# A two-layer hybrid trunk: three 256-column matmuls per weight block in place of a 512-column and a 256-column one, and no folds

## Chip, cores and metric

The kernel runs on one core of one Trainium2 chip. The metric is the device time of one execution in microseconds, from start to end; less is better. Three runs of the kernel before took 2072.51 to 2072.72 us, with a median of 2072.55 us.

## What is computed

Two residual layers on a stream x of 256 positions by 2048 features, in float32. The first mixes tokens by sparse attention over the keys that an indexer selects, the second by a gated short convolution; behind each stands a dense MLP with a squared ReLU. Cut to what matters here:

```python
x = x + dsa_mixer(rmsnorm(x), attn_w_in, attn_w_out)      # 2048 -> 4176, 2048 -> 2048
x = x + sqrelu_mlp(rmsnorm(x), mlp_w1[0], mlp_w2[0])      # 2048 -> 8192 -> 2048
x = x + short_conv_mixer(rmsnorm(x), conv_w_in, conv_w_out)  # 2048 -> 6144, 2048 -> 2048
x = x + sqrelu_mlp(rmsnorm(x), mlp_w1[1], mlp_w2[1])
```

Nearly all the work is in the products of activations with weights. All 389 MB of weights are read once.

## The kernel before

**Precision.** TensorE takes float32 operands in a fast form (fp32r). To keep accuracy, each operand is cut in two: a high part, the value rounded to that form, and a low part, what is left. A product is the sum of three: high by high, high by low and low by high. `split` (lines 215 to 237) does this for the weights: a ScalarE copy makes `wh` (line 231), a VectorE subtraction makes `wl` (line 232). Activations lie transposed, features on partitions; for each feature tile k there is a 512-column row `xk` with the 256 positions' high parts in columns 0 to 255 and their low parts in columns 256 to 511.

**Units, ticks and pieces.** The work is a fixed list of units, made by `add_unit` (lines 189 to 195) in the order of lines 942 to 1002. A unit is one strip of a weight matrix (up to 1104 columns wide) with its whole or partial contraction. It runs in ticks; each tick takes one piece, `kk` feature tiles of the strip. The main loop (lines 1059 to 1072) issues the matmuls of one piece, lets every live generator take one step (`step_all`; the generators are the ends of earlier units, norms, attention), and splits a later piece; the splits run four pieces ahead. The order of instructions on every engine is the order in which this Python code issues them.

**Wide units** (query, key, value and indexer projections, and the very last strip) hold a 128-position tile of the activations as the stationary operand and move 336 to 512 weight columns past it: three matmuls for each product, lines 258 to 260.

**Tall units**, all others, 116 of them, hold a 128x128 weight block as the stationary operand and move activations past it. Each has four blocks of columns, and a PSUM bank of 512 columns for each block. For each block and feature tile there are two matmuls:

```python
nc.tensor.matmul(o, wh, xk, start=(k == 0), stop=False)
nc.tensor.matmul(o[:, 0:256], wl, xk[:, 0:256], start=False, stop=(k == K - 1))
```

The first (line 253) moves all 512 columns past `wh`, so the bank's first half collects high by high and its second half high by low. The second (line 254) moves the 256 high columns past `wl` into the first half. There are 5248 such pairs (2816 with activations in the tile `xp`, 2432 in `hq`).

**Folds.** When a unit ends, the halves of its four banks are added: `fold` (lines 835 to 839) copies the second half to SBUF on ScalarE (tile `half`) and adds the first half to it on VectorE. `fold4` (lines 841 to 850) does it for the four banks, two in a step, and gives two SBUF tiles of 512 columns. Five ends call it: `add_to_xT` (the residual add), `h_gen` (squared ReLU), `c_end`, `y_gen` and `by_gen` (the convolution's three inputs). There are 464 folds.

PSUM has eight banks; up to three are taken by norms, attention and transposes, and units take theirs in turn.

Of the kernel before, what the change touches and what calls it, by code (L numbers as in the profile page):

```python
# [14 lines left out]
AF = mybir.ActivationFunctionType  # L15
ALU = mybir.AluOpType
AX = mybir.AxisListType

P = 128
# [54 lines left out]
def trunk(ctx: ExitStack, tc: tile.TileContext, x, positions, attn_norm_g, attn_w_in, attn_q_norm_g,  # L74
          attn_k_norm_g, attn_w_out, conv_norm_g, conv_w_in, conv_w, conv_w_out, mlp_norm_g,
          mlp_w1, mlp_w2, inv, out):
    nc = tc.nc
# [6 lines left out]
    def nm(s):  # L84
        cnt[0] += 1
        return f"{s}_{cnt[0]}"

    def sbt(shape, tag, bufs, dt=F32):
        return sb.tile(shape, dt, name=nm(tag), tag=tag, bufs=bufs)
# [5 lines left out]
    def tmp():  # L95
        return sbt([P, 512], "tmp", NTMP)
# [10 lines left out]
    def bank():  # L107
        return psum.tile([P, 512], F32, name=nm("ps"), tag="ps", bufs=8)
# [25 lines left out]
    def pause(n):  # L134
        for _ in range(n):
            yield

    def wait(*keys):
        while not all(k in done for k in keys):
            yield  # L140
# [98 lines left out]
    def matmuls(p):  # L239
        u, i, _ = pieces[p]  # L240
        n, K = u.n, u.kk * u.ticks
        if i == 0:
            u.banks = [[bank() for _ in u.widths] for _ in range(1 if u.tall else 2)]
        hi, lo = piece_tiles.pop(p)
        for t, row in enumerate(u.banks):
            c = 0
            for o, w in zip(row, u.widths):
                for j in range(u.kk):
                    k = i * u.kk + j
                    wh, wl = (v[:, j * n + c : j * n + c + w] for v in (hi, lo))  # L250
                    xk = u.lhs(k)
                    if u.tall:
                        nc.tensor.matmul(o, wh, xk, start=(k == 0), stop=False)  # L253
                        nc.tensor.matmul(o[:, 0:256], wl, xk[:, 0:256], start=False, stop=(k == K - 1))  # L254
                    else:
                        ah = xk[:, t * P : (t + 1) * P]
                        al = xk[:, 256 + t * P : 256 + (t + 1) * P]
                        nc.tensor.matmul(o[:, :w], ah, wh, start=(k == 0), stop=False)  # L258
                        nc.tensor.matmul(o[:, :w], al, wh, start=False, stop=False)  # L259
                        nc.tensor.matmul(o[:, :w], ah, wl, start=False, stop=(k == K - 1))  # L260
                c += w


# [143 lines left out]
    def start_norm(key, q):  # L407
        live.append(normT_gen(norms[key], q))
        if q == 3:
            live.append(rowsT_gen(norms[key]))  # L410
# [14 lines left out]
    def rows_of(key, power):  # L425
        return norms[key][power + "rows"].unsqueeze(1).to_broadcast([P, 2, 256])


    def add_to_xT(q, then=None):

        def gen(banks):
            r = yield from fold4(banks)
            for i in range(2):
                v = xT[q][:, i * 512 : (i + 1) * 512]
                nc.vector.tensor_tensor(v, v, r[i], ALU.add)  # L435
            r = None
            if then is not None:
                start_norm(then, q)

        return lambda banks: live.append(gen(banks))  # L440
# [383 lines left out]
    def put_pair(key, q, i, val):  # L824

        if i == 0:
            Q[key, q] = hq()
        v = Q[key, q].rearrange("p (j c) -> p j c", c=512)[:, 2 * i : 2 * i + 2]
        hi, lo = v[:, :, 0:256], v[:, :, 256:512]
        val = val.rearrange("p (j c) -> p j c", c=256)  # L830
        nc.scalar.activation(hi, val, AF.Copy)  # L831
        nc.vector.tensor_tensor(lo, val, hi.bitcast(F32), ALU.subtract)  # L832
        done.add((key, q, i))

    def fold(dst, ps):

        h = sbt([P, 256], "half", 4)
        nc.scalar.activation(h, ps[:, 256:512], AF.Copy)  # L838
        nc.vector.tensor_tensor(dst, ps[:, 0:256], h, ALU.add)  # L839

    def fold4(banks):
        row = list(banks[0])
        banks = None
        r = []
        for i in range(2):
            r.append(tmp())
            for j in range(2):
                fold(r[i][:, j * 256 : (j + 1) * 256], row.pop(0))
            yield
        return r  # L850


    def m1_end(key, q):
        def end(banks):
            live.append(h_gen(key, q, banks))

        return end

    def h_gen(key, q, banks):
        r = yield from fold4(banks)  # L860
        banks = None
        for i in range(2):
            nc.vector.scalar_tensor_tensor(r[i], r[i], 0.0, r[i], op0=ALU.max, op1=ALU.mult)
        yield from wait((key[:-1], "rows"))
        if q == 0:
            yield from pause(ROWS_PAUSE)
        for i in range(2):
            r3 = r[i].rearrange("p (j c) -> p j c", j=2)
            nc.gpsimd.tensor_tensor(r3, r3, rows_of(key[:-1], "rs2"), ALU.mult)  # L869
        yield  # L870
        for i in range(2):
            put_pair(key, q, i, r[i])
            yield


    C = {}

    def c_end(q):
        def gen(banks):
            C["c", q] = yield from fold4(banks)  # L880

        return lambda banks: live.append(gen(banks))

    def u_end(q):
        def end(banks):
            live.append(y_gen(q, banks))

        return end

    def b_end(q):  # L890
        def end(banks):
            live.append(by_gen(q, banks))

        return end

    def cw(j, k):
        return gT[:, 48 + j * 16 + k : 48 + j * 16 + k + 1]

    def y_gen(q, banks):
        u = yield from fold4(banks)  # L900
        banks = None
        yield from wait(("conv", "rows"))
        c = C.pop(("c", q))
        C["y", q] = []
        for i in range(2):
            z = u[i]
            z3 = z.rearrange("p (j c) -> p j c", j=2)
            nc.gpsimd.tensor_tensor(c[i].rearrange("p (j c) -> p j c", j=2),
                                    c[i].rearrange("p (j c) -> p j c", j=2), rows_of("conv", "rs2"), ALU.mult)
            nc.vector.tensor_tensor(z, z, c[i], ALU.mult)  # L910
            yield
            y = c[i]
            for j in range(2):
                k = q * 4 + 2 * i + j
                src, o = z[:, j * 256 : (j + 1) * 256], y[:, j * 256 : (j + 1) * 256]
                nc.scalar.activation(o, src, AF.Copy, scale=cw(2, k))
                for s in (1, 2):
                    nc.vector.scalar_tensor_tensor(
                        o[:, s:], src[:, : 256 - s], cw(2 - s, k), o[:, s:], op0=ALU.mult, op1=ALU.add
                    )  # L920
            C["y", q].append(y)
            yield
        done.add(("y", q))

    def by_gen(q, banks):
        b = yield from fold4(banks)
        banks = None
        yield from wait(("y", q), ("conv", "rows"))
        y = C.pop(("y", q))
        for i in range(2):  # L930
            b3 = b[i].rearrange("p (j c) -> p j c", j=2)
            nc.gpsimd.tensor_tensor(b3, b3, rows_of("conv", "rs"), ALU.mult)
            nc.vector.tensor_tensor(y[i], y[i], b[i], ALU.mult)
            put_pair("by", q, i, y[i])
            yield
# [85 lines left out]
    ps = bank()  # L1021
# [30 lines left out]
    ps = None  # L1052
# [6 lines left out]
    for p in range(len(pieces)):  # L1059
        matmuls(p)  # L1060
        u, i, _ = pieces[p]
        if i == u.ticks - 1:
            u.end(u.banks)
            u.banks = None
            if u.then is not None:
                live.append(u.then())
        step_all()
        while ahead < p + 1 + (AHEAD if p >= 6 else 2):
            split(ahead)
            ahead += 1  # L1070
        if p == 15:
            TP = 3
# [22 lines left out]
```

## Time and profile before

| | |
|---|---|
| median of three runs | 2072.55 us |
| profiled execution | 2071.95 us |
| its span (first to last instruction) | 2070.1 us |
| outside the span | 1.85 us |
| PE (matmul) busy | 2062.2 us, 100% of the span |
| PEld (weight load) busy | 1820.9 us, 88% |
| DVE (VectorE) busy | 1458.3 us, 70% |
| ACT (ScalarE) busy | 1056.9 us, 51% |
| POOL (GpSimd) busy | 298.2 us, 14% |
| share of the 16 DMA engines, weight queue | 58.7% |

Busy time of PE counts the time in which at least one matmul is under way, and matmuls overlap: a matmul's duration in the trace is longer than the distance to the next one's start. What a matmul costs in a stream is that distance, and it is read from the timeline, start to start, over many of them; the timeline rounds to 0.01 us.

### The profile page before, as it was taken

Reading aid. Unit: us, or ns where it says so; the run is one execution under the profiler, and the core shown is the slowest. Engines: PE = TensorE matmul, PEld = TensorE weight load, DVE = VectorE, ACT = ScalarE, POOL = GpSimd, SP = SyncE. Lnnn points to the kernel's source line nnn. Section 1 sums busy time; section 2 is a strip of 40 time slices with the busy share of each in tenths; the row PEclk is TensorE's granted clock in tenths of the full one; section 3 lists DMA queues with packets and bytes.
Section 4 is the critical chain, followed back from the end, with each engine's and each line's share of the span. In section 5 each row is a group of like instructions: output and inputs, shape, how many; then the busy total and the mean of one; then the engine's idle time right before and its main releaser. Section 6 shows DMA issues by size and latency. Waiting matters only on the chain.

```text
span 2070.1 us, 29937 instructions
## 1 busy us (share of the span) xinstructions
PE 2062.2 (100%) x11908; PEld 1820.9 (88%) x11908; DVE 1458.3 (70%) x1860; ACT 1056.9 (51%) x1549; POOL 298.2 (14%) x294
## 2 busy tenths in 40 slices
PE   9999999999999999999999999999999999999998
PEld 9888888888888888888888888888888888888887
DVE  6588877767667676677866676667676776767755
ACT  7456565545445454445645444555454544545443
POOL 1243105100101001010230110132010010100100
PEclk9999999999999999999999999999999999999999
DMA  8544456565665665655656555566656656665563
GB/s 301 163 149 157 145 186 199 192 195 186 201 200 187 196 191 190 198 188 197 203 180 201 188 192 193 189 195 194 197 186 201 192 195 186 201 200 187 187 192 110
DMA packets 191837, 392.87 MB, mean 190 GB/s; under 512 B 6752, under 2 KB 8016, under 8 KB 191696
## 3 DMA queue, kind: packets, MB, share of 16 engines
q1 hardware_dynamic: 191664, 390.94, 58.7%
q8 instruction: 93, 1.52, 0.3%
q14 instruction: 48, 0.39, 0.1%
q10 hardware_dynamic: 32, 0.01, 0.0%
HBM read 388.83 MB, written 2.10 MB: 189 GB/s over the span
## 4 chain that ended last, share of the span: by engine, by line
PE 99%; DVE 1%; POOL 0%; ACT 0%; issue 0%; DVEq 0%; POOLq 0%
PE ps L253 57%; PE ps L254 29%; PE ps L260 3%; PE ps L259 3%; PE ps L258 3%; PE ps L738 1%; PE ps L783 0%; PE ps L158 0%; PE ps L157 0%; PE ps L159 0%; PE ps L321 0%; PE ps L723 0%; PE ps L451 0%; PE ps L1023 0%; PE ps L384 0%; DVE hq L469 0%
## 5 line engine op out<-in xcount | busy, mean ns | idle before, releaser
L232 DVE TENSOR_TENSOR wl<-raw,wh 128x1024 fp32r<-128x1024 f32 (+2 forms) x738 | 945.6, 1284 | 377.5 <-ACT wh L231 374.4
L231 ACT ACTIVATE wh<-raw 128x1024 fp32r<-128x1024 f32 (+2 forms) x738 | 779.2, 1059 | 515.9 <-PE ps L253 442.5
L253 PE MATMUL ps<-xp,wh 128*128 128x512 f32 x2816 | 960.1, 389 | 0.0
L253 PE MATMUL ps<-hq,wh 128*128 128x512 f32 x2432 | 828.5, 389 | 0.0
L254 PE MATMUL ps<-xp,wl 128*128 128x256 f32 x2816 | 777.3, 276 | 0.0
L254 PE MATMUL ps<-hq,wl 128*128 128x256 f32 x2432 | 671.3, 276 | 0.0
L253 PEld LDWEIGHTS ps<-xp,wh 128*128 128x128 f32 x2816 | 528.6, 188 | 109.7
L253 PEld LDWEIGHTS ps<-hq,wh 128*128 128x128 f32 x2432 | 456.5, 188 | 94.6
L254 PEld LDWEIGHTS ps<-xp,wl 128*128 128x128 f32 x2816 | 528.7, 188 | 0.1
L254 PEld LDWEIGHTS ps<-hq,wl 128*128 128x128 f32 x2432 | 456.5, 188 | 0.1
L838 ACT ACTIVATE half<-ps 128x256 f32<-128x256 f32 x464 | 164.0, 382 | 280.2 <-PE ps L254 280.0
L839 DVE TENSOR_TENSOR tmp<-ps,half 128x256 f32<-128x256 f32 x464 | 183.6, 419 | 172.1 <-ACT half L838 171.9
L869 POOL TENSOR_TENSOR tmp<-tmp,tmp 128x512 f32<-128x512 f32 x64 | 123.6, 1950 | 1086.5 <-ACT wh L231 614.3
L258 PE MATMUL ps<-wh,xp 128*128 128x512 f32 (+2 forms) x288 | 108.8, 378 | 0.2 <-ACT wh L231 0.2
L260 PE MATMUL ps<-wl,xp 128*128 128x512 f32 (+2 forms) x288 | 106.6, 370 | 0.3 <-DVE wl L232 0.3
L259 PE MATMUL ps<-wh,xp 128*128 128x512 f32 (+2 forms) x288 | 106.7, 371 | 0.0
L435 DVE TENSOR_TENSOR xT<-xT,tmp 128x512 f32<-128x512 f32 x144 | 99.3, 731 | 0.0
L831 ACT ACTIVATE hq<-tmp 128x512 fp32r<-128x512 f32 x72 | 45.5, 632 | 96.8 <-POOL tmp L869 73.2
L832 DVE TENSOR_TENSOR hq<-tmp,hq 128x512 fp32r<-128x512 f32 x72 | 82.1, 1141 | 5.6 <-ACT hq L831 5.6
L373 POOL TENSOR_TENSOR tmp<-tmp,tmp 128x512 f32<-128x512 f32 x21 | 38.6, 1840 | 253.2 <-ACT tmp L372 184.9
L260 PEld LDWEIGHTS ps<-wl,xp 128*128 128x128 f32 x288 | 54.1, 188 | 8.4 <-DVE wl L232 0.7
L258 PEld LDWEIGHTS ps<-wh,xp 128*128 128x128 f32 x288 | 54.1, 188 | 7.5 <-ACT wh L231 0.4
(141 smaller groups left out, 764.3 us busy)
## 6 DMA issues: line engine op xcount, KB each, us to landing
raw<-in_mlp_w SPq DMA_DIRECT2D x256, 1024.0 KB, 5.4
raw<-in_conv_w_in SPq DMA_DIRECT2D x48, 1024.0 KB, 5.1
raw<-in_attn_w_in SPq DMA_DIRECT2D x24, 1024.0 KB, 5.4
raw<-in_attn_w_out SPq DMA_DIRECT2D x16, 1024.0 KB, 5.1
raw<-in_conv_w_out SPq DMA_DIRECT2D x16, 1024.0 KB, 5.1
raw<-in_attn_w_in SPq DMA_DIRECT2D x4, 1104.0 KB, 10.1
raw<-in_attn_w_in SPq DMA_DIRECT2D x7, 552.0 KB, 8.1
out_y<-hq SPq DMA_DIRECT2D x7, 256.0 KB, 2.8
```

Of the source, the lines that this page charges most:

```text
L231: nc.scalar.activation(hi[:, a], src[:, a], AF.Copy)
L232: nc.vector.tensor_tensor(lo[:, a], src[:, a], hi[:, a].bitcast(F32), ALU.subtract)
L253: nc.tensor.matmul(o, wh, xk, start=(k == 0), stop=False)
L254: nc.tensor.matmul(o[:, 0:256], wl, xk[:, 0:256], start=False, stop=(k == K - 1))
L258: nc.tensor.matmul(o[:, :w], ah, wh, start=(k == 0), stop=False)
L259: nc.tensor.matmul(o[:, :w], al, wh, start=False, stop=False)
L260: nc.tensor.matmul(o[:, :w], ah, wl, start=False, stop=(k == K - 1))
L435: nc.vector.tensor_tensor(v, v, r[i], ALU.add)
L832: nc.vector.tensor_tensor(lo, val, hi.bitcast(F32), ALU.subtract)
L838: nc.scalar.activation(h, ps[:, 256:512], AF.Copy)
L839: nc.vector.tensor_tensor(dst, ps[:, 0:256], h, ALU.add)
L869: nc.gpsimd.tensor_tensor(r3, r3, rows_of(key[:-1], "rs2"), ALU.mult)
```

## The change

In `matmuls`, a tall unit's block now gets three matmuls of 256 columns, all added into the same 256 columns: high activations past `wh`, low activations past `wh`, high activations past `wl`. Two blocks share a bank, each in a half, so a unit takes two banks where it took four. Only the first matmul into a bank, that of the even block, carries the start flag. With the sum complete in PSUM, `fold` and `fold4` are gone; `copy2` makes one ScalarE copy per bank into the same kind of SBUF tile, and the five ends call it. The tile `half` is gone; all other SBUF tiles stand where they stood. Wide units keep their three matmuls.

```diff
-            u.banks = [[bank() for _ in u.widths] for _ in range(1 if u.tall else 2)]
+            u.banks = [[bank() for _ in u.widths[:: 2 if u.tall else 1]] for _ in range(1 if u.tall else 2)]
         hi, lo = piece_tiles.pop(p)
+        if u.tall:
+            for c in range(len(u.widths)):
+                o = u.banks[0][c // 2][:, c % 2 * 256 : c % 2 * 256 + 256]
+                for j in range(u.kk):
+                    k = i * u.kk + j
+                    wh, wl = (v[:, j * n + c * P : j * n + (c + 1) * P] for v in (hi, lo))
+                    xk = u.lhs(k)
+
+                    for w, x, first, last in (
+                        (wh, xk[:, 0:256], k == 0 and c % 2 == 0, False),
+                        (wh, xk[:, 256:512], False, False),
+                        (wl, xk[:, 0:256], False, k == K - 1),
+                    ):
+                        nc.tensor.matmul(o, w, x, start=first, stop=last, skip_group_check=True)
+            return
...
-                    if u.tall:
-                        nc.tensor.matmul(o, wh, xk, start=(k == 0), stop=False)
-                        nc.tensor.matmul(o[:, 0:256], wl, xk[:, 0:256], start=False, stop=(k == K - 1))
...
-    def fold(dst, ps):
-
-        h = sbt([P, 256], "half", 4)
-        nc.scalar.activation(h, ps[:, 256:512], AF.Copy)
-        nc.vector.tensor_tensor(dst, ps[:, 0:256], h, ALU.add)
-
-    def fold4(banks):
+    def copy2(banks):
         row = list(banks[0])
         banks = None
         r = []
-        for i in range(2):
+        for _ in range(2):
             r.append(tmp())
-            for j in range(2):
-                fold(r[i][:, j * 256 : (j + 1) * 256], row.pop(0))
+            nc.scalar.activation(r[-1], row.pop(0), AF.Copy)
             yield
         return r
```

TensorE's order at the start of an MLP unit, before (ps is a PSUM bank, hq the activations, wh and wl the weight parts; each row is one matmul, its output 128 rows by the columns named):

```order
L253 MATMUL ps_9059<-hq_8020,wh_8975 128x512
L254 MATMUL ps_9059<-hq_8020,wl_8976 128x256
L253 MATMUL ps_9059<-hq_8020,wh_8975 128x512
L254 MATMUL ps_9059<-hq_8020,wl_8976 128x256
L253 MATMUL ps_9060<-hq_8020,wh_8975 128x512
L254 MATMUL ps_9060<-hq_8020,wl_8976 128x256
```

The same place with the change (x2 stands for two matmuls in a row with the same tiles):

```order
L258 MATMUL ps_10556<-hq_9278,wh_10453 128x256 x2
L258 MATMUL ps_10556<-hq_9278,wl_10454 128x256
L258 MATMUL ps_10556<-hq_9278,wh_10453 128x256 x2
L258 MATMUL ps_10556<-hq_9278,wl_10454 128x256
L258 MATMUL ps_10556<-hq_9278,wh_10453 128x256 x2
L258 MATMUL ps_10556<-hq_9278,wl_10454 128x256
```

The order of blocks and feature tiles is the same; the 512-column matmul has become two of 256 with the same `wh` block, and the third block goes into the first block's bank.

ScalarE's order at the end of a unit of the convolution, before (half holds a bank's second half, line 231 is the split of a later weight piece, line 916 the convolution's first tap):

```order
L231 ACTIVATE wh_10220<-raw_10065 128x1024
L838 ACTIVATE half_10241<-ps_10067 128x256
L838 ACTIVATE half_10244<-ps_10068 128x256
L231 ACTIVATE wh_10247<-raw_10065 128x1024
L838 ACTIVATE half_10274<-ps_10069 128x256
L838 ACTIVATE half_10277<-ps_10070 128x256
L231 ACTIVATE wh_10280<-raw_10118 128x1024
L231 ACTIVATE wh_10302<-raw_10118 128x1024
L916 ACTIVATE tmp_10054<-tmp_10240,gT 128x256 x2
```

The same place with the change (line 852 is the copy in `copy2`, line 920 the same tap):

```order
L231 ACTIVATE wh_11958<-raw_11754 128x1024
L852 ACTIVATE tmp_11986<-ps_11756 128x512
L231 ACTIVATE wh_11988<-raw_11754 128x1024
L852 ACTIVATE tmp_12020<-ps_11757 128x512
L231 ACTIVATE wh_12022<-raw_11816 128x1024
L231 ACTIVATE wh_12052<-raw_11816 128x1024
L920 ACTIVATE tmp_11748<-tmp_11986,gT 128x256 x2
```

Two copies of 256 columns have become one of 512 at the same place between the same splits; on VectorE the two additions that followed them are gone.

## Rows read from the trace of the kernel before

**Rows 1.** The page: span, busy time, granted clock, chain that ended last
```profile
span 2070.1 us, 29937 instructions
...
PE 2062.2 (100%) x11908; PEld 1820.9 (88%) x11908; DVE 1458.3 (70%) x1860; ACT 1056.9 (51%) x1549; POOL 298.2 (14%) x294
...
PEclk9999999999999999999999999999999999999999
...
PE 99%; DVE 1%; POOL 0%; ACT 0%; issue 0%; DVEq 0%; POOLq 0%
```

**Rows 2.** The page's groups: count | busy us, mean ns | idle before
```profile
L253 PE MATMUL ps<-xp,wh 128*128 128x512 f32 x2816 | 960.1, 389 | 0.0
L253 PE MATMUL ps<-hq,wh 128*128 128x512 f32 x2432 | 828.5, 389 | 0.0
L254 PE MATMUL ps<-xp,wl 128*128 128x256 f32 x2816 | 777.3, 276 | 0.0
L254 PE MATMUL ps<-hq,wl 128*128 128x256 f32 x2432 | 671.3, 276 | 0.0
...
L838 ACT ACTIVATE half<-ps 128x256 f32<-128x256 f32 x464 | 164.0, 382 | 280.2 <-PE ps L254 280.0
L839 DVE TENSOR_TENSOR tmp<-ps,half 128x256 f32<-128x256 f32 x464 | 183.6, 419 | 172.1 <-ACT half L838 171.9
```

**Rows 3.** Busy us by engine (instructions), PEclk, in two stretches of tall units
```profile
400.00:1000.00 600.00, 600.00 (x3531) 531.31 (x3530) 420.57 (x503) 298.09 (x424) 52.27 (x27) 1.00 0.60 193
1400.00:1980.00 580.00, 580.00 (x3413) 513.45 (x3412) 408.36 (x483) 286.70 (x404) 57.90 (x30) 1.00 0.61 194
```

**Rows 4.** PE's timeline inside a tall unit: start us, duration us
```profile
999.89 0.39 PE L253 MATMUL ps<-hq,wh 128*128 128x512 f32 x1
1000.12 0.28 PE L254 MATMUL ps<-hq,wl 128*128 128x256 f32 x1
...
1002.95 0.39 PE L253 MATMUL ps<-hq,wh 128*128 128x512 f32 x1
```

**Rows 5.** PE's timeline in the wide k and v unit
```profile
60.18 0.39 PE L258 MATMUL ps<-wh,xp 128*128 128x512 f32 x1
...
72.19 0.39 PE L260 MATMUL ps<-wl,xp 128*128 128x512 f32 x1
```

**Rows 6.** PE's timeline where tall units give way to a wide one
```profile
2020.91 0.40 PE L258 MATMUL ps<-wh,hq 128*128 128x512 f32 x1
...
2022.07 0.39 PE L260 MATMUL ps<-wl,hq 128*128 128x512 f32 x1
...
2022.98 0.39 PE L258 MATMUL ps<-wh,hq 128*128 128x512 f32 x1
```

**Rows 7.** PE's timeline: twelve transposes between tall matmuls
```profile
251.33 1.47 PE L783 MATMUL ps<-ident,tmp 128*128 128x128 f32 x12
252.56 0.48 PE L253 MATMUL ps<-hq,wh 128*128 128x512 f32 x1
```

**Rows 8.** PE's timeline: index scores, three 256-column matmuls in a row
```profile
99.75 0.28 PE L157 MATMUL ps<-tmp,tmp 128*128 128x256 f32 x1
99.86 0.28 PE L158 MATMUL ps<-tmp,tmp 128*128 128x256 f32 x1
99.98 0.28 PE L159 MATMUL ps<-tmp,tmp 128*128 128x256 f32 x1
100.10 0.40 PE L157 MATMUL ps<-tmp,tmp 128*128 128x512 f32 x1
```

**Rows 9.** PE's timeline in the wide indexer unit, one tick
```profile
43.70 0.34 PE L258 MATMUL ps<-wh,xp 128*128 128x384 f32 x1
...
46.72 0.34 PE L258 MATMUL ps<-wh,xp 128*128 128x384 f32 x1
```

**Rows 10.** A ScalarE copy of a whole bank (line groups)
```profile
L455 ACT ACTIVATE hq<-ps 128x512 f32<-128x512 f32 x8 | 4.8, 599 | 11.4 <-PE ps L451 11.4
```

**Rows 11.** Weight loads of line 1023, one stationary tile: duration ns min/median/max
```profile
L1023 PEld LDWEIGHTS ps<-ones x12: 288/333/333, 1.0 to 3.3; 128*128 128x128 f32 x12
```

More of the change, by code (lines that the diff above doesn't have):

```diff
@@ L251, in matmuls @@
                     xk = u.lhs(k)
-                    if u.tall:
-                        nc.tensor.matmul(o, wh, xk, start=(k == 0), stop=False)
-                        nc.tensor.matmul(o[:, 0:256], wl, xk[:, 0:256], start=False, stop=(k == K - 1))
[L255 to L260, printed above, removed]
+                    ah = xk[:, t * P : (t + 1) * P]
+                    al = xk[:, 256 + t * P : 256 + (t + 1) * P]
+                    nc.tensor.matmul(o[:, :w], ah, wh, start=(k == 0), stop=False)
+                    nc.tensor.matmul(o[:, :w], al, wh, start=False, stop=False)
+                    nc.tensor.matmul(o[:, :w], ah, wl, start=False, stop=(k == K - 1))
                 c += w
@@ L431, in gen @@
         def gen(banks):
-            r = yield from fold4(banks)
+            r = yield from copy2(banks)
             for i in range(2):
@@ L859, in h_gen @@
     def h_gen(key, q, banks):
-        r = yield from fold4(banks)
+        r = yield from copy2(banks)
         banks = None
@@ L879, in gen @@
         def gen(banks):
-            C["c", q] = yield from fold4(banks)
+            C["c", q] = yield from copy2(banks)
         return lambda banks: live.append(gen(banks))
@@ L899, in y_gen @@
     def y_gen(q, banks):
-        u = yield from fold4(banks)
+        u = yield from copy2(banks)
         banks = None
@@ L925, in by_gen @@
     def by_gen(q, banks):
-        b = yield from fold4(banks)
+        b = yield from copy2(banks)
         banks = None
```

## The prediction

> **What bounds the kernel now.** I read the page's engine shares and the chain of waits first, then the busy time of two long stretches, then TensorE's own timeline, start to start. The page says which engine to look at: PE is busy in 2062.2 of 2070.1 us, the chain that ended last is 99% PE, and the granted clock is full in every slice [rows 1]. VectorE (70%) and ScalarE (51%) have room. The 7.9 us in which PE is not busy cannot be in the body of the work: in two stretches of 600 and 580 us of tall units PE is busy for all of it [rows 3]. So in the tall units nothing but the matmuls' own pace sets the time: no wait for a split, a bank or a fold is left there. The groups' durations (389 and 276 ns) are of no use for a price, since matmuls overlap [rows 2]; the pace is.
>
> The pace of a pair: nine pairs lie between the starts at 999.89 and 1002.95, 3.06 us or 340.0 ns each [rows 4]. Over 600 us there are 3531 matmuls, of which one or so only reaches over an edge: some 1765 pairs of 339.9 ns; over 580 us, 3413 and 340.0 ns [rows 3]. I take 340.0, good to 0.15. The 5248 pairs [rows 2] are 1784 us, 86% of the span.
>
> The pace by columns: in a wide unit 53 windows of 512 columns lie between 60.18 and 72.19, 226.6 ns each, good to 0.2 [rows 5]. If the 512-column matmul of a pair takes as long (the rounded 0.23 us from 999.89 to 1000.12 fits [rows 4]), 113.4 ns are left for the 256-column one. That is 0.443 ns for a column in both: a matmul costs its columns and nothing else.
>
> **The change, part by part.**
>
> *Matmuls.* A block and feature tile moved 512 + 256 = 768 columns and now moves 3 x 256 = 768. By the paces above three short windows are 3 x 113.4 = 340.2 ns against 340.0: +0.2 ns, and with 5248 of them +1 us. The error comes from the two paces: the difference is 2 x 340.0 less 3 x 226.6, which is good to 2 x 0.15 + 3 x 0.2 = 0.9 ns, so this term lies between -0.7 and +1.1 ns, or -4 and +6 us.
>
> *Weight loads.* Each matmul has a load of its own before and after, even where the stationary tile stays the same: loads and matmuls are both 11908 [rows 1], and line 1023's six matmuls with one stationary tile have their loads each [rows 11]. So 5248 loads come on top. What hides them is the matmul ahead of each. Before, a load of `wl` had a window of 226.6 ns and the load of the next `wh` one of 113.4, and the pair ran at its columns' pace: a load with 113.4 ns to itself costs nothing. With the change every load has 113.4 ns. For two of the three (a `wh` load beside high activations) this is the old short window word for word; the third (the `wl` load, now beside the 256 low columns alone) is new, and so are short windows in an unbroken row. I take nothing for it, by the nearest row, the tall pair itself; the other end comes from the rows of the first rival, +10 to +15 ns a block.
>
> *Folds and copies.* 464 additions of 419 ns leave VectorE (194 us), 464 copies of 382 ns leave ScalarE (177 us) and 232 copies of a whole bank come in [rows 2]; the back transposes' copy out of a full bank takes 599 ns [rows 10], so 139 us. All of it lies beside PE's work and none on the path; I cost it at nothing. The first result tile was there one copy and one addition after the second bank closed (0.80 us) and is now there 0.60 us after the first bank, with the same two blocks in it, closes: no reader is later. If this cover went, the price would be a bank's wait at a unit's start; a unit with four ticks of eight products runs 32 x 0.34 = 10.9 us, its copies 1.2, and it takes two banks where it took four. No DMA, split or POOL step is moved past another: the copies stand between the same splits as the folds did.
>
> *Sum.* 2071.95 us for the profiled execution (2070.1 of span and 1.85 around it) + 1 + 0 + 0 = 2073 us. The median of the runs is 0.6 us above that execution, which is inside the term's error. **Forecast: 2073 us, no change** that a measurement could tell; one of this kernel can tell about 0.2%, 4.1 us, from none. By the errors of the paces alone this case runs from 2067 to 2078.
>
> **Rivals.**
>
> *First, slower: a load no longer fits under a short window once short windows follow one another.* The place is the new row of 256-column windows; it decides as soon as a load, from the moment its place is free, takes over 113.4 ns, and nothing of 226.6 ns is left in which to catch up. For it: the only unbroken row of 256-column fp32r matmuls in this trace, three in the index scores. The first, behind a 512-column window, takes 0.11 us, the next two 0.12 each, and all three 0.35 [rows 8]: 10 ns over 340, so 5248 x 10 = +52 us, 2125. The indexer's wide unit runs above its columns' pace too: a tick of twelve windows of 384 and six of 336 columns, 6624 columns, should take 2.93 us and takes 3.02 [rows 9], 4.9 ns a window, so 3 x 4.9 x 5248 = +77 us, 2150. If only the new kind of window pays, the `wl` load's, with the 5 to 7 ns that separate 0.12 from 0.113, it is +26 to +37 us, 2099 to 2110. Against it: such slow windows also follow every change of stream, and with 512 columns, where a load has time to spare. Where tall units give way to a wide one, five windows take 1.16 us, 232 each, and the next four 0.91, 227.5 [rows 6]. The three short windows stand right behind such a change and the indexer's unit, whose width changes every few windows, never runs undisturbed; a tall unit does nothing else for hundreds of windows. I give this rival 0.33: 0.22 for all windows (about 2125 to 2150), 0.11 for the new kind alone (about 2105).
>
> The Trainium skill bears on it ("TensorE: Matmul & The Clock Gate", section "LDWEIGHTS (loading the stationary operand)"): a load of 128 columns takes 128/1.2, an estimate of 107 ns. By that rule it would fit and this rival would cost nothing; the tall pairs agree with it, the 0.12 us of [rows 8] do not.
>
> *Second, slower: a fixed price for each matmul.* 5248 matmuls more would each pay it. The paces say 0.2 ns, at most 1.1; at that end it is +5.8 us, 2078, just outside no change. That takes both rounding errors at their worst: 0.03.
>
> The Trainium skill ("TensorE: Matmul & The Clock Gate", section "Back-to-back issue gap") states such a price, N/2.4 + 2.5 ns for N columns; by it the change would cost 5248 x 2.5 = 13 us, 2086. The rows disagree: its 216 ns for 512 columns is 226.6 here, and no constant is left beside the columns [rows 4, 5].
>
> *Third, slower still: instructions come too slowly.* PE takes four instructions (two loads, two matmuls) in 340 ns now, 85 ns each, and would take six, 57 each. A run of twelve transposes, 24 instructions, gets from 251.33 to 252.56, 51 ns each [rows 7], but that is a burst. At 60 ns in the long run a block would take 360, +105 us, 2178. 0.03.
>
> *Fourth, faster: the lighter VectorE and ScalarE give PE something back.* There is nothing to give in tall units [rows 3], and the 7.9 us without PE work stand outside them. To gain over 4.1 us, the paces would have to be off by their whole error the other way. 0.06, at about 2068.
>
> *Fifth: the repeated load is not done.* If the second load of the same `wh` were left out, PEld would count 11908 as before. The first rival would lose one load of three, and the time would be the forecast's, since the columns set the pace; it is part of that case.
>
> **How the numbers follow.** The forecast's case holds 0.55. Slower by over 0.2%: 0.33 + 0.03 + 0.03 = 0.39. Faster by over 0.2%: 0.06. The time is the likeliest case's, 2073. The range goes down to 2067, the forecast's lower error, and up to 2145, which takes in the rival's new kind alone and most of its all-windows case; left out are the upper end of that case and the third rival above, some 0.10, and a little below. The likeliest case's own range is 2067 to 2078.
>
> **What would show it.** Right: PE's timeline in a tall unit starts a matmul every 0.113 us, nine triples in 3.06 us; PE and PEld count 17156 each; still 100% PE busy in stretches like 400 to 1000 us; VectorE's busy time down by some 194 us, ScalarE's by some 38; no new wait of PE on `copy2`'s copies. Wrong: triples at 350 to 360 ns in the body of a unit (first rival: all three windows long, or only the one in which `wl` is loaded), any PE idle time before a unit's first matmul (banks), or a triple below 339.

## The result, and the profile after

The changed kernel takes **2140.36 us** (median of 4 runs, 2140.25 to 2140.63); the kernel before took 2072.53 beside it (4 runs, 2071.94 to 2072.72). The ratio is 1.0327 with a 95% interval of 1.0315 to 1.0339: slower by 67.8 us, where 2073 and no change were forecast. Spread over the 5248 blocks that is 12.9 ns each.

From the page of the changed kernel: span, busy time by engine, granted clock in the 40 slices, the chain that ended last.

```profile
span 2138.7 us, 39669 instructions
...
PE 2132.1 (100%) x17156; PEld 2095.2 (98%) x17156; DVE 1293.2 (60%) x1396; ACT 1031.6 (48%) x1317; POOL 294.1 (14%) x294
...
PEclk9999999999999999999999999999999999999999
...
PE 99%; DVE 1%; POOL 0%; issue 0%; ACT 0%; DVEq 0%; POOLq 0%
```

Against [rows 1] the picture is the same: the chain is 99% PE and the clock is full in every slice. PE is not busy for 6.6 us (7.9 before), so no new wait is in it. All that grew is PE's busy time: 2062.2 to 2132.1, +69.9 us, with 5248 more matmuls and as many more loads. VectorE and ScalarE have become lighter. PE's waits in the trace are the same four lines as before, 2.4 us in all.

The page's groups for the matmuls of the tall units and for the copy that took the folds' place (count | busy us, mean ns | idle before), answering to [rows 2]:

```profile
L258 PE MATMUL ps<-xp,wh 128*128 128x256 f32 x5632 | 997.4, 280 | 0.0
L258 PE MATMUL ps<-hq,wh 128*128 128x256 f32 x4864 | 860.7, 280 | 0.0
L258 PE MATMUL ps<-xp,wl 128*128 128x256 f32 x2816 | 796.2, 283 | 0.0
L258 PE MATMUL ps<-hq,wl 128*128 128x256 f32 x2432 | 687.5, 283 | 0.0
...
L852 ACT ACTIVATE tmp<-ps 128x512 f32<-128x512 f32 x232 | 138.0, 595 | 348.3 <-PE ps L258 348.3
```

These durations overlap and give no pace: a window (one matmul and the columns that it moves) of 256 columns is listed with 280 to 283 ns here and with 276 before, while three of them follow one another in 353. The two stretches that answer to [rows 3] do (busy us of PE, PEld, DVE, ACT, POOL, each with its instructions; clock; DMA share; GB/s):

```profile
400.00:1000.00 600.00, 600.00 (x5097) 600.00 (x5096) 346.76 (x318) 275.31 (x320) 50.09 (x26) 1.00 0.57 187
1400.00:1980.00 580.00, 580.00 (x4924) 579.89 (x4923) 339.18 (x314) 267.56 (x314) 66.74 (x42) 1.00 0.57 186
```

PE is busy throughout, as before, at the full clock (1.00). 5097 matmuls are 1699 blocks, 353.1 ns each; 4924 are 1641.3, 353.4 each. Before it was 339.9 and 340.0. So **the pace of a block went from 340 to 353 ns, and PE waits for nothing that the profile shows**: 5248 x 13.1 is 69 us, the whole loss. TensorE's own timeline of the changed kernel inside the tall unit of [rows 4] (start us, duration; x2 is two matmuls shown as one):

```profile
1000.12 0.40 PE L258 MATMUL ps<-hq,wh 128*128 128x256 f32 x2
1000.35 0.28 PE L258 MATMUL ps<-hq,wl 128*128 128x256 f32 x1
...
1002.94 0.28 PE L258 MATMUL ps<-hq,wh 128*128 128x256 f32 x1
```

Eight blocks lie between 1000.12 and 1002.94, 352.5 ns each. Over all 5248 blocks the trace's starts give a mean of 115.6 ns for the high activations past `wh`, 117.3 for the low ones past `wh` and 120.8 for the high ones past `wl`, where the columns alone would take 113.3: each of the three is long.

### The profile page after: what moved, and what is told of

Its sections match the earlier page's. It is cut to its first block, busy times and chain, and to the rows that moved or that the text cites. A ratio compares the mean times of both kernels' runs of the same rounds, so it can differ in the third digit from the quotient of the medians.

```text
span 2138.7 us, 39669 instructions
## 1 busy us (share of the span) xinstructions
PE 2132.1 (100%) x17156; PEld 2095.2 (98%) x17156; DVE 1293.2 (60%) x1396; ACT 1031.6 (48%) x1317; POOL 294.1 (14%) x294
## 4 chain that ended last, share of the span: by engine, by line
PE 99%; DVE 1%; POOL 0%; issue 0%; ACT 0%; DVEq 0%; POOLq 0%
PE ps L258 87%; PE ps L271 3%; PE ps L270 3%; PE ps L269 3%; PE ps L749 0%; PE ps L794 0%; PE ps L158 0%; PE ps L157 0%; PE ps L159 0%; PE ps L332 0%; PE ps L734 0%; PE ps L462 0%; PE ps L1027 0%; PE ps L395 0%; DVE hq L480 0%
## 5 line engine op out<-in xcount | busy, mean ns | idle before, releaser
L258 PE MATMUL ps<-xp,wh 128*128 128x256 f32 x5632 | 997.4, 280 | 0.0
L258 PEld LDWEIGHTS ps<-xp,wh 128*128 128x128 f32 x5632 | 867.4, 188 | 0.2
L258 PE MATMUL ps<-hq,wh 128*128 128x256 f32 x4864 | 860.7, 280 | 0.0
L258 PE MATMUL ps<-xp,wl 128*128 128x256 f32 x2816 | 796.2, 283 | 0.0
L258 PEld LDWEIGHTS ps<-hq,wh 128*128 128x128 f32 x4864 | 748.9, 188 | 0.2
L258 PE MATMUL ps<-hq,wl 128*128 128x256 f32 x2432 | 687.5, 283 | 0.0
L852 ACT ACTIVATE tmp<-ps 128x512 f32<-128x512 f32 x232 | 138.0, 595 | 348.3 <-PE ps L258 348.3
L384 POOL TENSOR_TENSOR tmp<-tmp,tmp 128x512 f32<-128x512 f32 x21 | 38.4, 1830 | 267.1 <-ACT tmp L383 196.3
L269 PEld LDWEIGHTS ps<-wh,xp 128*128 128x128 f32 x288 | 54.1, 188 | 7.7 <-ACT wh L231 0.4
L270 PEld LDWEIGHTS ps<-wh,xp 128*128 128x128 f32 x288 | 54.2, 188 | 7.1
```

What stands on the lines that cost most here:

```text
L258: nc.tensor.matmul(o, w, x, start=first, stop=last, skip_group_check=True)
L384: nc.gpsimd.tensor_tensor(st["acc"], st["acc"], sq, ALU.add)
L852: nc.scalar.activation(r[-1], row.pop(0), AF.Copy)
```

## The experiments

Four theories, by the letters that the expectations use. **A**, the prediction's first rival: a weight load takes longer than a short window and shows. **B**: a fixed price for each matmul. **C**: the load of the next block and the columns that stream beside it get in each other's way, by where the two lie in SBUF; "place" below is where a tile or block begins in SBUF, counted in bytes. **D**: PE's instructions can't come faster than some rate. Beside them stands whether the folds had anything to do with it. The two benches ran once, for their trace; all other kernels ran for an interval.

### e1: the pace of a row, by columns and by place

Behind the last instruction of the kernel before, rows of 48 equal matmuls: first with fewer and fewer moving columns, with both tiles at the same place modulo 2048 B; then 256 columns with the stationary block shifted by 64 B a row; then narrower stationary blocks; last 512 and 256 columns in turn.

```diff
+    S, M = (sbt([P, 512], "tmp", NTMP, F32R) for _ in range(2))
...
+    for _ in range(48): nc.tensor.matmul(pb[0:128, 0:256], S[:, 0:128], M[:, 0:256], start=True, stop=True)
...
+    for _ in range(48): nc.tensor.matmul(pb[0:128, 0:256], S[:, 16:144], M[:, 0:256], start=True, stop=True)
...
+    for _ in range(48): nc.tensor.matmul(pb[0:64, 0:256], S[:, 0:64], M[:, 0:256], start=True, stop=True)
```

> The kernel before, with rows of matmuls added behind its last instruction, 48 of each kind, on tiles of their own: moving widths 512 down to 128 columns, 256 columns with the stationary block moved by 64 bytes at a time (15 steps), 256 columns with a stationary block of 64 and of 32 columns, and 512 and 256 columns in turn. Theory A (a weight load needs about 118 ns, and a row of 256-column windows has nothing to catch up in): 118 ns for every width of 256 and below, the columns' 0.443 ns each from 272 columns (120 ns) up, and 113 ns for 256 columns with a stationary block of 64. Theory B (each matmul pays some 4.5 ns while its stream is not of 512-column windows alone or mixed with them, as 384 and 336 columns did before): 118 at 256, 175 at 384, 153 at 336, and no gain from a smaller block. Theory C (the load and the moving columns get in each other's way by where they lie in SBUF): the 15 steps differ, some at 113 and some at 120. Theory D (instructions come at no more than two in 118 ns): 118 for 256 columns and below whatever the block's size, 113 nowhere below 266 columns.

TensorE's timeline of this kernel behind the old end (start us, duration of the 48 together); a row's pace is its start to the next row's start, over 48:

```profile
2064.47 11.04 PE L1078 MATMUL ps<-tmp,tmp 128*128 128x512 f32 x48
2075.35 9.89 PE L1079 MATMUL ps<-tmp,tmp 128*128 128x448 f32 x48
2085.08 8.48 PE L1080 MATMUL ps<-tmp,tmp 128*128 128x384 f32 x48
...
2120.15 5.92 PE L1085 MATMUL ps<-tmp,tmp 128*128 128x256 f32 x48
2125.91 5.50 PE L1086 MATMUL ps<-tmp,tmp 128*128 128x192 f32 x48
2131.25 5.50 PE L1087 MATMUL ps<-tmp,tmp 128*128 128x128 f32 x48
2136.58 5.67 PE L1088 MATMUL ps<-tmp,tmp 128*128 128x256 f32 x48
2142.09 5.85 PE L1089 MATMUL ps<-tmp,tmp 128*128 128x256 f32 x48
2147.78 5.81 PE L1090 MATMUL ps<-tmp,tmp 128*128 128x256 f32 x48
2153.43 5.91 PE L1091 MATMUL ps<-tmp,tmp 128*128 128x256 f32 x48
2159.18 5.82 PE L1092 MATMUL ps<-tmp,tmp 128*128 128x256 f32 x48
2164.83 5.86 PE L1093 MATMUL ps<-tmp,tmp 128*128 128x256 f32 x48
...
2221.70 5.61 PE L1103 MATMUL ps<-tmp,tmp 128*64 128x256 f32 x48
2227.14 5.60 PE L1104 MATMUL ps<-tmp,tmp 128*32 128x256 f32 x48
2232.58 8.64 PE L1105 MATMUL ps<-tmp,tmp 128*128 128x512 f32 x48
```

512 columns: 10.88/48 = 226.7 ns. 256 at the same place: 5.76/48 = 120.0, the slow window of the changed kernel. 192 and 128 columns both take 111 (5.34 and 5.33 over 48): there the load sets the pace, and **111 ns is under the 113.3 of 256 columns, so a load fits**. One line shows that a row need lose nothing: L1088 is the row of L1085 with the stationary block 64 B further, the same 48 instructions and columns, and it takes 5.51/48 = 114.8 with its first window, 113.3 from start to start once it runs. The other fourteen shifts take 117.7 to 120.0: 118.5 at 128 B, 117.7 at 192, 119.8 at 256, and so on every 256 B. But at 320 B, which by that count is the place of L1088, the row takes 5.65/48 = 117.7 (L1092), and so do 576 and 832 B. L1088 alone is entered from a row of 128 columns, and its first window lasts 171 ns. So this bench shows that the same instructions run at 113.3 or at up to 120, and not yet whether the place or the way into the row decides. With a stationary block of 64 or 32 columns at the old place it is 113.3 (5.44/48) as well, in one row each. The last row, 512 and 256 columns in turn at one place, takes 356 ns a pair, where the kernel's pairs take 340.0: a pair isn't safe either.

So D falls (113.3 with the same count of instructions), and B too (113.3 is half of 226.7, with nothing left over). A falls as it was put: the load is short enough, and it is late only in some rows. 448 columns, where a load has 198 ns, still take 202.7 and 384 take 173.4 for 170.0: what is lost is not a load that doesn't fit, but 3 to 7 ns in a window at every width tried from 256 to 448. The widths other than 256 ran at one place only, so that place has a part in their loss is not shown. C is left, for the next runs to test.

### e2: only the long matmul cut in two

The kernel before with its 512-column matmul as two of 256; four banks and the folds stay.

```diff
-                        nc.tensor.matmul(o, wh, xk, start=(k == 0), stop=False)
+                        nc.tensor.matmul(o[:, 0:256], wh, xk[:, 0:256], start=(k == 0), stop=False, skip_group_check=True)
+                        nc.tensor.matmul(o[:, 256:512], wh, xk[:, 256:512], start=False, stop=(k == K - 1), skip_group_check=True)
...
```

> The kernel before with only the 512-column matmul cut in two of 256 columns, four banks and the folds as before. If the loss is all in the short windows, 2140 us within 2 us, with blocks at 353 to 354 ns. If the missing folds, the shared banks or the adding into one half have a part in it, less: 2072 to 2130.

2141.09 us (2141.04 to 2141.28), ratio 1.0331 (1.0314 to 1.0348). The first of the two stretches:

```profile
400.00:1000.00 600.00, 600.00 (x5096) 600.00 (x5096) 403.62 (x479) 284.62 (x400) 50.38 (x26) 1.00 0.58 187
```

5096 matmuls where the changed kernel has 5097, with the folds still on VectorE (403.62 us for 346.76). Cutting the matmul is the whole loss; that two blocks share a bank, and the folds, add nothing to it.

### e3: the folds' addition left out

The kernel before with each fold cut to a copy of the first half; it leaves out the addition of the low activations' products.

```diff
-        h = sbt([P, 256], "half", 4)
-        nc.scalar.activation(h, ps[:, 256:512], AF.Copy)
-        nc.vector.tensor_tensor(dst, ps[:, 0:256], h, ALU.add)
+        nc.scalar.activation(dst, ps[:, 0:256], AF.Copy)
```

> The kernel before with its pairs of 512 and 256 columns, and folds cut to a ScalarE copy of the bank's first half; leaves out the addition of the second half (the high-by-low product). If folds are hidden, 2072.5 us within 1 us, VectorE's busy time lower by some 190 us. If they hold TensorE up somewhere, faster by over 4 us.

2071.62 us (2071.28 to 2072.6), ratio 0.9995 (0.9986 to 1.0005). Its page:

```profile
PE 2062.6 (100%) x11908; PEld 1821.7 (88%) x11908; DVE 1293.1 (62%) x1396; ACT 1058.0 (51%) x1549; POOL 295.3 (14%) x294
```

VectorE lost 165.2 us and the time did not move: the folds' additions were wholly hidden. Their ScalarE copies stay in this run; e7 below has no fold at all and is no faster either.

### e4: the map of places

Behind the kernel before, where the other engines are done but for VectorE's last 0.8 us, on a tall unit's own buffers (`wh`, `wl` and two `xp` tiles): sixteen blocks of three short windows, eight windows of 512 columns ahead of each, for eight shifts `a` of the `wh` block and eight `b` of the `wl` block, 64 B apart; then some pairs of 512 and 256 columns.

```diff
...
+        nc.tensor.matmul(pb[:, 0:256], H[:, a + o : a + o + 128], x[:, 0:256], start=True, stop=True)
+        nc.tensor.matmul(pb[:, 0:256], H[:, a + o : a + o + 128], x[:, 256:512], start=True, stop=True)
+        nc.tensor.matmul(pb[:, 0:256], W[:, b + o : b + o + 128], x[:, 0:256], start=True, stop=True)
...
```

> The kernel before, with rows of matmuls added behind its last instruction that copy a tall unit's: blocks of three 256-column windows from the weight tiles' own buffers, with the high weights moved by 0 to 448 bytes and the low ones by 0 to 448 (64 combinations of 64 bytes, 16 blocks each), and eight combinations for pairs of 512 and 256 columns; eight 512-column windows ahead of each row. Theory C (load and stream get in each other's way by where they lie): blocks between 340 and 360 ns by combination, 0 and 0 near 353; for pairs 0 and 0 at 340, high weights moved by 64 bytes near 353. Theory A (the load's time alone): all 64 within 2 ns of each other. Theory B (a price per matmul in such streams): the same.

TensorE's timeline for the first two places and, from a later window of it, for a third; L1087 is the first window of sixteen blocks, and the row of 512 columns behind it their end:

```profile
2065.66 2.00 PE L1097 MATMUL ps<-xp,wh 128*128 128x512 f32 x8
2067.49 0.28 PE L1087 MATMUL ps<-xp,wh 128*128 128x256 f32 x1
...
2073.14 1.99 PE L1099 MATMUL ps<-xp,wh 128*128 128x512 f32 x8
2074.97 0.28 PE L1087 MATMUL ps<-xp,wh 128*128 128x256 f32 x1
...
2080.42 1.99 PE L1101 MATMUL ps<-xp,wh 128*128 128x512 f32 x8
...
2126.80 0.28 PE L1087 MATMUL ps<-xp,wh 128*128 128x256 f32 x1
...
2132.55 2.00 PE L1115 MATMUL ps<-xp,wh 128*128 128x512 f32 x8
```

As the kernel has them (no shift): 5.65/16 = 353 ns, the changed kernel's pace to the nanosecond. `wl` 64 B further, nothing else changed: 5.45/16 = 341. `wh` 64 B further instead: 5.75/16 = 359. The whole map, worked out the same way from the trace, in ns a block:

| `wh` shift | `wl` +0 B | +64 B | +128 B | +192 B |
|---|---|---|---|---|
| +0 B | 353 | **341** | 348 | 353 |
| +64 B | 360 | 354 | 357 | 353 |
| +128 B | 353 | **340** | 355 | **341** |
| +192 B | 355 | 356 | 356 | 351 |

Shifts of 256 to 448 B repeat these within 1.5 ns, so the pattern has a period of 256 B. In the three bold cells the last eight blocks run at exactly 340.0, the columns' own pace. The pairs were a miss of the bench: with no shift it gives 349.9 ns, where the same pair at the same places runs at 340.0 in the kernel [rows 4], and with `wl` 256 B further, by the map the same place, it gives 340.9. The pace of a row also hangs on how it is entered, so the map points to places, and only the whole kernel decides.

### e5 and e10: the kernel before, one part moved by 64 B

If places matter, the kernel before was fast because its places suit its pairs, and a shift must make it slow without any short window. e5 moves `wh`, e10 moves `wl`.

```diff
-        a, b = (0, 0) if u.tall else (16, min(64, WPITCH - w))
+        a, b = (16, 0) if u.tall else (16, min(64, WPITCH - w))
```

> The kernel before with one change: in tall units the high weights lie 64 bytes further on in their buffer. Theory C: the pairs lose their pace, as the bench's pairs of equal places did (353 ns), 5248 x 13 = +68 us, 2141, or part of that. Theories A and B: 2072.5 within 1 us.

```diff
-        a, b = (0, 0) if u.tall else (16, min(64, WPITCH - w))
+        a, b = (0, 16) if u.tall else (16, min(64, WPITCH - w))
```

> The kernel before with the low weights 64 bytes further on in tall units, the place that suits the short windows. Theory C with the bench's pairs (353.2 ns at that place): 2072 + 5248 x 13 = 2141 us; less if the kernel's own stream finds its pace where the bench's did not, as it does at 0 and 0. Theories A and B: 2072.5.

e5: 2122.82 us, ratio 1.0243 (1.0226 to 1.0260). e10: 2107.06, ratio 1.0167 (1.0152 to 1.0183). The two stretches of e5:

```profile
400.00:1000.00 600.00, 600.00 (x3399) 520.51 (x3398) 403.72 (x480) 284.25 (x400) 50.36 (x26) 1.00 0.58 187
1400.00:1980.00 580.00, 580.00 (x3347) 507.32 (x3346) 398.16 (x472) 281.41 (x397) 66.74 (x41) 1.00 0.59 189
```

and of e10:

```profile
400.00:1000.00 600.00, 600.00 (x3464) 528.33 (x3463) 411.51 (x490) 288.93 (x407) 50.48 (x26) 1.00 0.59 190
1400.00:1980.00 580.00, 580.00 (x3347) 510.68 (x3346) 399.71 (x468) 278.96 (x389) 67.86 (x42) 1.00 0.59 190
```

A pair takes 2 x 600/3399 = 353.0 ns in the first stretch of e5 and 346.6 in the second; 346.4 and 346.6 in e10. Both lost only part of the 13 ns a pair that the bench had let expect, e10 half of it. Not an instruction was added: the same matmuls, the same loads, PE busy throughout, and the pace of the changed kernel in the worst stretch. In e5 the 512-column windows are long too (a mean of 234.1 ns from start to start, 227.0 in the kernel before; 115.9 for the short ones): even a load with 226 ns to itself costs the stream, so it is not its length. The kernel before ran at 340.0 by its places.

Between the two paces of e5 lies a step and no drift. TensorE's timeline on both sides of the one place where it changes; L384 is four matmuls of a norm's row sums:

```profile
1058.15 0.28 PE L254 MATMUL ps<-xp,wl 128*128 128x256 f32 x1
...
1065.22 0.28 PE L254 MATMUL ps<-xp,wl 128*128 128x256 f32 x1
1065.34 1.03 PE L384 MATMUL ps<-tmp,ones 128*128 128x256 f32 x4
...
1066.78 0.28 PE L254 MATMUL ps<-xp,wl 128*128 128x256 f32 x1
...
1073.72 0.28 PE L254 MATMUL ps<-xp,wl 128*128 128x256 f32 x1
```

Twenty pairs take 7.07 us ahead of it, 353.5 ns each, and twenty take 6.94 behind it, 347.0 each, with the same tiles on either side. By the trace's starts the pace is 353.3 in every part from 260 to 1065 us and 346.7 from there to 2046. So the places don't fix one pace. As far as these runs show, they decide which paces a stream can hold, and the way in, behind other matmuls, decides between them. In all ten whole kernels the long stretches between such interruptions run at one of three paces, 340.0, 346.7 or 353.3 ns. Why these three is not shown.

### e9: the kernel before, one part moved by 256 B

```diff
-        a, b = (0, 0) if u.tall else (16, min(64, WPITCH - w))
+        a, b = (0, 64) if u.tall else (16, min(64, WPITCH - w))
```

> The kernel before with the low weights 256 bytes further on in tall units. The bench's blocks repeat every 256 bytes, so Theory C in that form says no change, 2072.5 within 2 us; if the way back to the pace depends on more than the place modulo 256, up to 2090.

2072.14 us, ratio 0.9999 (0.9990 to 1.0008). So it is not the shift itself: 64 B cost 1.7%, 256 B nothing, as the map's period says.

### e6, e7 and e8: the changed kernel at the three good places

```diff
-        a, b = (0, 0) if u.tall else (16, min(64, WPITCH - w))
+        a, b = (32, 16) if u.tall else (16, min(64, WPITCH - w))
```

> The changed kernel with one more change: in tall units the high weights lie 128 bytes and the low ones 64 bytes further on, so that each stationary block begins 64 bytes behind the moving columns modulo 512, the place that ran at 113 ns a window in the first bench. Theory C: blocks at 340 to 345 ns, 2072 to 2100 us. Theories A and B: 2140 within 2 us.

```diff
-        a, b = (0, 0) if u.tall else (16, min(64, WPITCH - w))
+        a, b = (0, 16) if u.tall else (16, min(64, WPITCH - w))
```

> The changed kernel with only the low weights 64 bytes further on in tall units, the smallest move that ran at 340.0 ns a block in the bench of places. Theory C: 2072 to 2076 us. Theories A and B: 2140.

```diff
-        a, b = (0, 0) if u.tall else (16, min(64, WPITCH - w))
+        a, b = (32, 48) if u.tall else (16, min(64, WPITCH - w))
```

> The changed kernel with the high weights 128 and the low ones 192 bytes further on, the third combination at 340.0 in the bench; its first blocks behind the 512-column rows were slower there than the other two's. Theory C: 2073 to 2077 us, a little slower than the one with 0 and 64 bytes. Theories A and B: 2140.

| kernel | us | against the kernel before |
|---|---|---|
| e6: `wh` +128 B, `wl` +64 B | 2074.64 | 1.0011 (1.0002 to 1.0021) |
| e7: `wl` +64 B | 2072.05 | 0.9998 (0.9989 to 1.0007) |
| e8: `wh` +128 B, `wl` +192 B | 2071.33 | 0.9995 (0.9986 to 1.0003) |

The page and the two stretches of e7, which differs from the changed kernel by 64 B in one tile's place and nothing else:

```profile
PE 2063.1 (100%) x17156; PEld 2026.1 (98%) x17156; DVE 1292.8 (62%) x1396; ACT 1030.4 (50%) x1317; POOL 297.4 (14%) x294
```

```profile
400.00:1000.00 600.00, 600.00 (x5297) 600.00 (x5296) 361.62 (x335) 287.83 (x339) 52.04 (x27) 1.00 0.59 194
1400.00:1980.00 580.00, 580.00 (x5120) 580.00 (x5120) 353.24 (x324) 277.26 (x323) 58.62 (x31) 1.00 0.59 194
```

5297/3 and 5120/3 blocks are 339.8 ns each, in both stretches: all 68 us are back, with all 17156 matmuls and loads. e6 has one matmul fewer in the first stretch (x5296) and takes 2.6 us more. Some 5% of its short windows take 116 to 121 ns, and 96% of these lie ahead of 341 us: there it steps like e5, behind four matmuls of the same kind.

```profile
333.13 0.28 PE L258 MATMUL ps<-xp,wl 128*128 128x256 f32 x1
...
340.20 0.28 PE L258 MATMUL ps<-xp,wl 128*128 128x256 f32 x1
340.31 1.03 PE L395 MATMUL ps<-tmp,ones 128*128 128x256 f32 x4
...
341.42 0.28 PE L258 MATMUL ps<-xp,wl 128*128 128x256 f32 x1
...
347.88 0.28 PE L258 MATMUL ps<-xp,wl 128*128 128x256 f32 x1
```

Twenty blocks take 353.5 ns each ahead of them, nineteen 340.0 behind them. e7 does it too, for two short stretches between 232 and 251 us (356 ns). The changed kernel settles at 340.0 behind none of its interruptions. e8 was expected a little behind e7 and came 0.7 us ahead, inside both intervals. None of them beats the kernel before by what can be told here (0.2%); the change is worth nothing even at good places, and 3.3% against it at the places it was written for.

## Where the prediction was right, and where it was wrong

**What bounds the kernel: right.** PE's pace and nothing else, before and after: 99% of the chain, full clock, no wait.

***Matmuls*: right.** Three short windows cost their 768 columns: +0.2 ns a block was forecast with an error of about 1 either way, and e7 runs at 339.8 with the same matmuls. The second rival, a price for each matmul, is out by the same row. The 2.5 ns that the Trainium skill ("TensorE: Matmul & The Clock Gate", section "Back-to-back issue gap") puts on top of a matmul's columns, there for a matmul by itself, show in no row of e1 or e7. Charged to each of 5248 more matmuls they would put e7, by estimate, 13 us over the kernel before, and it is 0.2 under.

***Weight loads*: here it failed.** "I take nothing for it, by the nearest row, the tall pair itself": the pair showed a load with 113.4 ns to itself that cost nothing, and I took that for a property of the time it had. It was one of the places, and of how the stream came to them. The same pair 64 B off takes 346 or 353 ns (e10, e5), so the row that carried the term held for one layout and one order of windows only. The term was 0 and measured 12.9 ns a block, between the +10 and +15 that stood as its other end; hence the time lies in the range, which took in this rival at a chance of 0.33, but far outside the likeliest case.

**The first rival: right in its size, wrong in its reason.** It gave 2125 to 2150, all windows long, no new wait, triples of 350 to 360 ns; the trace shows 353 and all three long. But a load does not take over 113.4 ns: it takes 111 (e1), and three short windows in a row hold the columns' pace for hundreds of blocks once `wl` moves (e7). That three windows of the index scores gave the right size is in part luck: they used other tiles and were entered another way. The Trainium skill's 107 ns for it (same page, section "LDWEIGHTS (loading the stationary operand)") is near the 111 measured, so page and row agree that a load fits; by that rule nothing was lost, and 68 us were.

The evidence was in the rows and I set it aside. I called the slow windows of [rows 6], [rows 8] and [rows 9] the mark of streams that had just changed. e1 shows two of these widths slow in undisturbed rows of 48: 384 columns at 173.4 for 170.0, 256 at 120.0. A change of stream does matter, but as a step: the pace that follows it can hold to the next one (e5, e6). I should have asked what slow windows with 512, 384 and 256 columns had in common; it could not be the load's time, since 512 leave twice that.

What names the cause: same instructions, 64 B apart, both ways (e7 faster by 68 us than the changed kernel, e10 slower by 35 than the kernel before), with a period of 256 B (e4, e9). In e4 the same paces show with no other engine at work. And a smaller load at the bad place costs nothing (e1, one row each of 64 and 32 columns). So a load and the columns that stream beside it disturb each other by place, and among the paces that a place allows the way in decides; that it is their reads of SBUF that meet is a reading that fits, and no run shows it. The Trainium skill speaks against that reading ("TensorE: Matmul & The Clock Gate", section "Step-by-step: what each phase is for"): "Loading the next tile's weights doesn't steal SBUF read bandwidth from the running matmul." If a load cost the running matmul nothing in any way, e5 would have run at 2072; it took 2122.82, and the measurement decides. Whether bandwidth is what is lost, or something else that the two share, is not shown. Nor is it told apart whether the place of the block alone counts or its distance from the activations: the activations weren't moved.

***Folds and copies*: right.** The additions were hidden before (e3), nothing of the folds is missed without them (e7), and no bank is waited for. ScalarE's copies measured 138.0 us for the 139 forecast, 595 ns each for 599. The side sums were off: ScalarE fell by 25.3 us where I said 38, VectorE by 165.1 where I said 194. I had multiplied the groups' means by their counts; the groups' own busy times [rows 2] give 164.0 - 138.0 = 26.0 for ScalarE and 183.6 for VectorE, which leaves 18 unexplained there. None of it touches the time.

**The third and fifth rivals.** Instructions do not come too slowly: six in 339.8 ns (e7), 57 each. Every repeated load is done: PEld counts 17156. (The line of [rows 11] has 12 matmuls in the trace for its 12 loads, not the six that I counted in the program.) **The fourth**, a gain: VectorE 165 us lighter gave back nothing (e3, e7).

## What to carry to other kernels

Where PE is busy without a gap and still slower than its columns, look at the start-to-start time of single windows, and before blaming a load's or an instruction's price, move one operand by 64 B: a shift of an offset is the cheapest experiment there is, and here it was worth 3.3%. A pace read from a tuned row holds for its layout and its order of windows; a change that reorders windows or adds loads has to find its places again, so predict it with the places as a risk of their own. Where the pace steps behind a foreign matmul, places are suspect too. And a bench of sixteen blocks finds the candidates, but only the whole kernel shows which of them holds.

## What the runs showed of the hardware that was not expected

- A load beside a stream costs the stream 3 to 7 ns a window or nothing, by the places of the two in steps of 64 B with a period of 256 B: 340.0 to 360 ns a block of three windows (e4), 340.0, 346.4 and 353.0 a pair (kernel before, e10, e5). Long windows pay too: 234.1 for 227.0 (e5).
- A row of 128- or 192-column windows, each with a load of 128x128, goes at 111 ns a window, the load's own pace (e1).
- The pace of the same blocks at the same places hangs on what ran ahead: 349.9 a pair in the bench and 340.0 in the kernel with no shift; 117.7 and 113.3 a window 256 B apart (e1).
- A long stream runs at one of three paces, 340.0, 346.7 or 353.3 ns a block, and holds it until other matmuls come between: e5 steps from 353.3 to 346.7 at 1065 us, e6 from 353.3 to 340.0 at 340 us. What picks the pace is open.
